# Own buffers for the first gate's second half of weights, and one ordering edge less, in a hybrid encoder block

## The chip, the cores and the metric

The kernel runs on one core of one Trainium2 chip. The metric is the time of one execution on the device in microseconds (us), taken over several runs; a separate profiled execution gives the trace. The engines are TensorE (PE; its weight loads are shown as PEld), VectorE (DVE), ScalarE (ACT), GpSimd (POOL) and SyncE (SP), which issues most of the DMA transfers.

## The reference, cut to what matters

A sequence of 1024 frames with 16 learned meta tokens ahead of it runs through one block: a token mixer with two groups of heads, then a gated MLP with a causal depthwise convolution, each added to the stream, and a last norm.

```python
h = concatenate([meta, x], axis=1)                     # (1, 1040, 1024)
h = h + token_mixer(rmsnorm(h, norm_mix_g), ...)
h = h + channel_mixer(rmsnorm(h, norm_ffn_g), ...)
return rmsnorm(h, norm_final_g)[:, 16:]

def channel_mixer(u, w_up, w_gate, ffn_conv_w, w_down):   # D_FF = 2816
    a = causal_dwconv(u @ w_up, ffn_conv_w)               # 3 taps
    return (silu(a) * (u @ w_gate)) @ w_down
```

The change lies at the start of channel_mixer: the norm of its input and the products with the first block of w_up and w_gate.

## The kernel before

Everything is held transposed: features on the 128 partitions, time along the free axis. The residual stream lies in eight blocks of 128 features (RES; tiles resid). Every float32 operand of a product is split into a high part that TensorE reads in one pass (fp32r, made by a cast on ACT) and the rest (lo, made by a subtraction on DVE), and each product is three matmuls: hi by hi, hi by lo, lo by hi (mm3s, lines 924 to 926). All weights go through wsplit: a cast on line 783, a subtraction on line 784.

The 22 blocks of 128 columns of D_FF are taken in eleven pairs. For pairs 1 to 10 the products follow Strassen's scheme with seven half-size products (seven; its products are named pup_x, pup_y, pup_z for w_up and pga_x, pga_y, pga_z for w_gate), which needs sums and differences of the input's quarters: the combinations. Pair 0 is done in the ordinary way (eight), before the combinations are there. A name such as pup_001 is the product of w_up for block 0 of pair 0, half 0 of the time, part 1; pga_11 that of w_gate for block 1, half 1.

The stretch around the change, in the order of the code:
- The last quarter of the token mixer's output product (pwy) is added to the stream in two pieces of 256 columns. The squares of each piece (sqb) are summed over the blocks (Rb, line 2060). The norm of a piece is a matmul that sums over the partitions (pcb, line 827), a square root and a reciprocal on two columns, a matmul that spreads the result over rows (prb, line 839) and a copy to Rb (line 843). Then scale_tasks multiplies the eight blocks by Rb (line 2070) and makes the split input: uh_g and x on ACT (line 1998), ul_g and x on DVE (line 1999). Half 1, the later half of the time, has had its norm before (tiles xh, xl).
- first_up and first_gate compute pair 0: half 1 first, then half 0 in two parts, 0 (columns up to 256) and 1 (the rest).
- xcomb(k, j0, j1) makes the combinations for one of four feature blocks k and one part of the columns; the first quarter's have j0 = 0. Each has an ACT scaling (line 2025), subtractions on DVE (lines 2026, 2029, 2031, 2034) and four splits (xput: lines 1995 to 1999) into uh_g, ul_g, xh and xl. Its temporaries are xu, xt, xv.
- Then come the pairs; conv takes the up-projection's blocks through three taps and Silu (lines 2238 to 2241, tiles cv), and gate multiplies by the gate's block (line 2283).

The order of instructions on each engine here is made by a scheduler in the framework, which runs the program against a model of its own and keeps to the dependencies. `after(a, b)` adds an edge for the order only. Buffers come from pools; a tile waits until the readers of the one that had its place are done. Three places matter:
- Split weights take turns in a ring of three pairs of tiles of 128x1024 (split_tiles: hi, lo). fstep(u, s) makes the s-th split of the u-th weight block; u = 0 is w_up and u = 1 w_gate of pair 0, and s is the block of 128 columns. hi_ga_1 and lo_ga_1 in the order below are the splits for (u, s) = (1, 1). The raw weights of w_gate are the tiles fraw_ga.
- ctile gives tiles of 128x512 from a ring of six with the tag "cv"; before the change only the convolutions use it. Its pool is opened where the pool with the tiles rr has just been closed, whose last readers are matmuls of pwy.
- xcomb orders the first subtraction of every combination except the very first behind the last scaling of the stream (last["scaled"], set on line 2071 by xsingle).

## Time and profile before

| | |
|---|---|
| median of 3 runs | 1526.14 us (1525.41 to 1527.58) |
| span of the profiled execution | 1523.9 us; the profile states no time for it beside the span |
| median less that span | 2.2 us |
| PE busy | 1487.8 us, 98% of the span |
| PEld, DVE, ACT, POOL busy | 1349.9, 1090.4, 756.4, 72.1 us |
| granted clock of TensorE over the span | 0.995 |
| transfers | 223.81 MB, mean 147 GB/s |
| chain that ended last | PE 89%, DVE 5%, ACT 2%, DMA 2%, issue 1% |

The span runs from the first to the last instruction; a run's time has what lies around it as well. A busy time is the union of an engine's instructions. In a row of the timeline stand the start, the time, the engine, the line, the operation with what it writes and reads, and in brackets the idle time of the engine before it and what ended that. The end of a matmul is modelled, so its length is more than its distance to the next one's start. In the list of waits stand the total, the number of times and the longest. The chain of waits is followed back from the end, each step with its start and length.

### The profile page before, as it was taken

The numbers are of one execution on the slowest core, as the hardware profiler recorded it, in microseconds if no ns is written. First come the engines' busy times: TensorE is split into PE (matmuls) and PEld (weight loads), VectorE is DVE, ScalarE is ACT, GpSimd is POOL, SyncE is SP. The second block draws the span as 40 slices with busy tenths as digits, with TensorE's granted clock in tenths as the row PEclk, the third lists the DMA queues.
The fourth block names the chain that finished last, engine by engine and source line by source line (L and its number), as shares of the span: only waits on it lengthen the run. The fifth ranks groups of instructions, "written<-read, shape, count | busy, mean of one in ns | idle before, by whom it ended". The sixth has DMA issues, their size and how long they took to land.

```text
span 1523.9 us, 25488 instructions
## 1 busy us (share of the span) xinstructions
PE 1487.8 (98%) x9929; PEld 1349.9 (89%) x9929; DVE 1090.4 (72%) x2087; ACT 756.4 (50%) x1455; POOL 72.1 (5%) x157
## 2 busy tenths in 40 slices
PE   7989999999999999999999999999999999999997
PEld 7988999998999999987888998999999999888887
DVE  6885868677777677756867787766666666778667
ACT  4465655554655455544454565444444444344443
POOL 1000000000000000000000001222220000000000
PEclk9999999999999999999999999999999999999999
DMA  6022245323632446697333247887772224933213
GB/s 232 2 93 56 90 155 192 111 84 111 200 106 98 131 161 199 194 401 258 108 115 125 77 136 222 209 211 201 177 186 77 83 82 157 369 106 108 97 42 111
DMA packets 104586, 223.81 MB, mean 147 GB/s; under 512 B 10520, under 2 KB 33760, under 8 KB 104288
## 3 DMA queue, kind: packets, MB, share of 16 engines
q1 hardware_dynamic: 89824, 191.68, 37.4%
q0 software_dynamic: 8448, 23.07, 7.6%
q10 hardware_dynamic: 6192, 7.41, 1.4%
q8 instruction: 78, 1.28, 0.3%
q14 instruction: 44, 0.36, 0.1%
HBM read 178.05 MB, written 67.15 MB: 161 GB/s over the span
## 4 chain that ended last, share of the span: by engine, by line
PE 89%; DVE 5%; ACT 2%; DMA 2%; issue 1%; SPq 0%; DVEq 0%; ACTq 0%
PE pdx L926 3%; PE pdx L925 3%; PE pdx L924 3%; PE pup_x L925 2%; PE pup_x L924 2%; PE pup_x L926 2%; PE pga_x L924 2%; PE pga_x L925 2%; PE pga_x L926 2%; PE pdy L926 2%; PE pdy L925 2%; PE pdy L924 2%; PE n L1621 2%; PE pwx L926 2%; PE u L1619 2%; PE pwx L924 2%
## 5 line engine op out<-in xcount | busy, mean ns | idle before, releaser
L783 ACT CAST hi_up<-raw_up 128x512 fp32r<-128x512 f32 (+1 forms) x52 | 36.4, 719 | 106.7 <-PE pga_z L925 60.2
L924 PE MATMUL pup_x<-uh_g,hi_up 128*128 128x256 f32 (+1 forms) x240 | 67.6, 284 | 1.2 <-ACT uh_g L1995 1.2
L784 DVE TENSOR_TENSOR lo_up<-raw_up,hi_up 128x512 fp32r<-128x512 f32 (+1 forms) x52 | 41.3, 809 | 38.3 <-ACT hi_up L783 37.5
L784 DVE TENSOR_TENSOR lo_ga<-fraw_ga,hi_ga 128x512 fp32r<-128x512 f32 (+1 forms) x52 | 41.9, 808 | 37.3 <-ACT hi_ga L783 37.1
L925 PE MATMUL pup_x<-ul_g,hi_up 128*128 128x256 f32 (+1 forms) x240 | 67.7, 284 | 0.1
L926 PE MATMUL pup_x<-uh_g,lo_up 128*128 128x256 f32 (+1 forms) x240 | 66.5, 283 | 0.0
L784 DVE TENSOR_TENSOR lo_d<-rd,hi_d 128x1024 fp32r<-128x1024 f32 (+1 forms) x34 | 37.7, 1113 | 32.8 <-ACT hi_d L783 32.7
L783 ACT CAST hi_ga<-fraw_ga 128x512 fp32r<-128x512 f32 (+1 forms) x52 | 36.4, 719 | 45.5 <-PE pup_z L925 24.1
L926 PE MATMUL pdx<-uh_d,lo_d 128*128 128x512 f32 (+1 forms) x156 | 57.9, 375 | 0.0
L925 PE MATMUL pdx<-ul_d,hi_d 128*128 128x512 f32 (+1 forms) x156 | 57.8, 374 | 0.0
L783 ACT CAST hi_d<-rd 128x1024 fp32r<-128x1024 f32 (+1 forms) x34 | 32.3, 959 | 49.3 <-PE pdy L925 32.5
L926 PE MATMUL pdy<-uh_d,lo_d 128*128 128x512 f32 x132 | 51.9, 393 | 0.0
L925 PE MATMUL pdy<-ul_d,hi_d 128*128 128x512 f32 x132 | 51.7, 392 | 0.0
L924 PE MATMUL pdx<-uh_d,hi_d 128*128 128x512 f32 (+1 forms) x156 | 48.5, 372 | 0.0
L924 PE MATMUL pdy<-uh_d,hi_d 128*128 128x512 f32 x132 | 47.9, 389 | 0.0
L924 PEld LDWEIGHTS pup_x<-uh_g,hi_up 128*128 128x128 f32 x240 | 45.7, 191 | 2.3 <-ACT uh_g L1995 1.4
L924 PE MATMUL pga_x<-uh_g,hi_ga 128*128 128x512 f32 x120 | 47.5, 396 | 0.0
L925 PE MATMUL pga_x<-ul_g,hi_ga 128*128 128x512 f32 x120 | 47.5, 396 | 0.0
L926 PE MATMUL pga_x<-uh_g,lo_ga 128*128 128x512 f32 x120 | 47.1, 393 | 0.0
L925 PEld LDWEIGHTS pup_x<-ul_g,hi_up 128*128 128x128 f32 x240 | 45.8, 191 | 1.0 <-DVE ul_g L1996 0.3
L926 PEld LDWEIGHTS pup_x<-uh_g,lo_up 128*128 128x128 f32 x240 | 45.0, 190 | 0.7
L1688 DVE SCALAR_TENSOR_TENSOR mx<-tr,vec,sig 128x386 f32<-128x386 f32 (+2 forms) x42 | 24.0, 571 | 21.1 <-PE tr L1680 16.0
(1687 smaller groups left out, 5732.4 us busy)
## 6 DMA issues: line engine op xcount, KB each, us to landing
raw_up<-w_up_d SPq DMA_DIRECT2D x22, 512.0 KB, 5.6
fraw_ga<-w_gate_d SPq DMA_DIRECT2D x22, 512.0 KB, 4.3
acts<-cv SPq DMA_DIRECT2D x44, 256.0 KB, 4.6
wsd<-w_down_d POOLq DMA_DIRECT2D x44, 256.0 KB, 6.7
rd<-wsd SPq DMA_DIRECT2D x22, 512.0 KB, 3.5
raw_w<-w_out_d SPq DMA_DIRECT2D x20, 512.0 KB, 7.3
wsw<-raw_w SPq DMA_DIRECT2D x32, 256.0 KB, 3.1
raw_m<-w_out_d SPq DMA_DIRECT2D x14, 512.0 KB, 4.0
```

Of the source, the lines that this page charges most:

```text
L783: AC.copy(hi[:, o:o + n], x)
L784: V.tensor_tensor(lo[:, o:o + n], x, hi[:, o:o + n].bitcast(F32), ALU.subtract)
L924: m.append(PE.matmul(pt, ah, xh_, start=first and k == 0, stop=False, skip_group_check=True))
L925: PE.matmul(pt, ah, xl_, start=False, stop=False, skip_group_check=True)
L926: m.append(PE.matmul(pt, al, xh_, start=False, stop=last and k == n - 1, skip_group_check=True))
L1619: PE.matmul(up[:, :nv], kw[:L], v, start=True, stop=True)
L1621: PE.matmul(pn[:L, :nv], pt[:L, :L], v, start=True, stop=c == 0)
L1688: return V.scalar_tensor_tensor(dst, tr[:, x0 - t0:x1 - t0], vec[:, g:g + 1], sig(b, p)[:, x0 - a0:x1 - a0], ALU.mult, ALU.mult)
```

## The change

The split for (u, s) = (1, 1), the second block of columns of pair 0's gate, no longer takes a place in the ring of weight tiles. It is made in two pieces of 512 columns, hi and lo each, in four tiles from the ring "cv" (higa_1_0, higa_1_1, loga_1_0, loga_1_1). Products of eight read the piece that holds their columns. And the edge in xcomb holds only for the second part of the columns (j0 > 0).

```diff
@@ fsplit, wsplit @@
+    def wsplit2(nm, x):
+        r = [[ctile(f"{p}{nm}_{i}", F32R) for i in range(2)] for p in ("hi", "lo")]
+        for i in range(2):
+            wsplit(r[0][i], r[1][i], [x[:, i * HB:(i + 1) * HB]])
+        return r
+
@@ fstep @@
+        if (u, s) == (1, 1):
+            return wsplit2(nm, r1)
         if u < 2:
             return fsplit(nm, [(r0, r1)[s]])
@@ xcomb @@
         x = V.scalar_tensor_tensor(t3, B1, g1, u4, ALU.mult, ALU.subtract)
-        if k or j0:
+        if j0:
             after(x, last["scaled"])
@@ eight @@
-            mm3s(pt, [tuple(y[:, kb * P:(kb + 1) * P] for y in (hi, lo)) for kb in range(KB)],
+            mm3s(pt, [tuple(y[kb // 4][:, kb % 4 * P:(kb % 4 + 1) * P] if type(y) is list else y[:, kb * P:(kb + 1) * P] for y in (hi, lo)) for kb in range(KB)],
                  [tuple(y[:, kb % 4, j0:j1] for y in xs[kb]) for kb in range(KB)], True, True)
```

The scheduler moves instructions by it on PE, DVE and ACT between the norm of the two last pieces and the products of pair 1; on SP one load moves; the rest of the program stands in the order of before. Lines from 788 on have numbers higher by 6 to 8 in the changed kernel.

On ACT, at the split of the first block of the gate's weights (hi_ga_0), before:

```order
L783 CAST hi_ga_0_9731<-fraw_ga_0_9422 128x1024
L2056 ACTIVATE sqb_3_9464<-resid_8123 128x256
L2056 ACTIVATE sqb_5_9504<-resid_8124 128x256
L2056 ACTIVATE sqb_6_9508<-resid_8125 128x256
L2056 ACTIVATE sqb_7_9512<-resid_8125 128x256
```

and in the changed kernel:

```order
L783 CAST hi_ga_0_9731<-fraw_ga_0_9422 128x1024
L783 CAST higa_1_0_9847<-fraw_ga_1_9424 128x512
L783 CAST higa_1_1_9848<-fraw_ga_1_9424 128x512
L2064 ACTIVATE sqb_3_9464<-resid_8123 128x256
L2064 ACTIVATE sqb_5_9504<-resid_8124 128x256
```

The casts of the second block stand ahead of the squares of the two last pieces; before, that cast (hi_ga_1) stood 31 rows further on, behind the scaling of both pieces. On DVE the two subtractions loga_1_0 and loga_1_1 likewise stand behind lo_ga_0 and ahead of the sums in Rb.

On PE, at the end of pga_01, the gate's product for block 0 and half 1, before:

```order
L926 MATMUL pga_01_9855<-xh_9052,lo_ga_0_9732 128x512
L924 MATMUL pup_000_9911<-uh_g,hi_up_0_9418 128x256
L924 MATMUL pup_100_9938<-uh_g,hi_up_1_9426 128x256
L925 MATMUL pup_000_9911<-ul_g,hi_up_0_9418 128x256
L926 MATMUL pup_000_9911<-uh_g,lo_up_0_9419 128x256
```

and in the changed kernel (pcb_9633 is the norm's sum for the last piece):

```order
L934 MATMUL pga_01_9859<-xh_9052,lo_ga_0_9732 128x512
L932 MATMUL pga_11_9887<-xh_9054,higa_1_0_9847 128x512
L933 MATMUL pga_11_9887<-xl_9055,higa_1_0_9847 128x512
L934 MATMUL pga_11_9887<-xh_9054,loga_1_0_9849 128x512
L835 MATMUL pcb_9633<-cs,Rb 128x1 x2
```

The 24 matmuls of pga_11 come directly behind pga_01. Before, they came behind pup_000, pup_100, pup_001 and pup_101, mixed with pga_00. Now the order behind them is pup_000 (with prb of the last piece after its first 12 matmuls), pup_100, pga_00, pga_10, pup_001, pup_101.

On DVE, at the last combinations of the second part (k = 3), around the product of the first convolution of pair 1 with its gate (cv_00<-s0ga,cv_00), before:

```order
L2283 TENSOR_TENSOR cv_00_10314<-s0ga_10339,cv_00_10314 128x512
L2026 SCALAR_TENSOR_TENSOR xt_256_10225<-resid_8123,vec,xv_256_10211 128x258
L2034 SCALAR_TENSOR_TENSOR xv_256_10211<-resid_8125,vec,xv_256_10211 128x258
L2029 SCALAR_TENSOR_TENSOR xt_256_10225<-resid_8123,vec,xt_256_10225 128x258
L2031 TENSOR_TENSOR xv_256_10211<-resid_8123 128x258
```

and in the changed kernel:

```order
L2034 SCALAR_TENSOR_TENSOR xt_256_10229<-resid_8123,vec,xv_256_10215 128x258
L2004 TENSOR_TENSOR ul_g<-xv_256_10215,uh_g 128x258
L2291 TENSOR_TENSOR cv_00_10318<-s0ga_10343,cv_00_10318 128x512
L2037 SCALAR_TENSOR_TENSOR xt_256_10229<-resid_8123,vec,xt_256_10229 128x258
L2039 TENSOR_TENSOR xv_256_10215<-resid_8123 128x258
L2042 SCALAR_TENSOR_TENSOR xv_256_10215<-resid_8125,vec,xv_256_10215 128x258
```

The first xt now stands ahead of that product, and one of the two xv has gone behind the second xt. On ACT, between the cast hi_up_3 of pair 1 and the load of the Silu table for that convolution stood one scaling, one cast and one copy (uh_g, uh_g, s2up); now one cast stands there (uh_g).

## The prediction

> **What bounds the kernel now.** I read the page first, then the list of PE's waits from 760 us on, then the busy times by stretches around the place that the change touches (columns after the stretch: PE, PE's weight loads, DVE, ACT, POOL, then the granted clock, the DMA share and GB/s).

> ```profile
> span 1523.9 us, 25488 instructions
> PE pup L925 <- DVE ul_g L1999: 1.7, 1, 1.7
> PE pup_x L924 <- ACT uh_g L1995: 1.2, 1, 1.2
> PE pga L924 <- ACT hi_ga L783: 0.8, 1, 0.8
> 870.00:875.00 5.00, 3.33 (x27) 3.00 (x25) 3.20 (x10) 3.11 (x8) 0.00 (x0) 1.00 0.00 0
> 880.00:885.00 5.00, 4.22 (x34) 3.93 (x33) 3.85 (x6) 2.00 (x2) 0.00 (x0) 1.00 0.22 57
> 915.00:920.00 5.00, 3.67 (x20) 3.09 (x19) 3.45 (x10) 2.43 (x7) 0.00 (x0) 0.83 0.90 301
> 920.00:925.00 5.00, 5.00 (x38) 5.00 (x37) 3.86 (x8) 2.30 (x5) 0.00 (x0) 0.83 0.55 211
> 930.00:1400.00 470.00, 470.00 (x2763) 415.68 (x2762) 324.78 (x497) 205.65 (x357) 52.37 (x74) 1.00 0.60 168
> ```

> TensorE is the bound: from 930 to 1400 us it is busy for all 470.00 us. So what the change can be worth is what PE loses between about 845 and 930 us, the start of the gated MLP. There it waits three times, and after the third wait the clock is 0.83 in two stretches of 5 us, which are 10 x 0.17 = 1.7 us lost. The column of idle time understates a stall, because the end of the matmul ahead of it is modelled. Start to start is the honest measure:

> ```profile
> 872.83 0.51 PE L924 MATMUL pup<-uh_g,hi_up 128*128 128x258 f32 x2
> 875.03 0.39 PE L925 MATMUL pup<-ul_g,hi_up 128*128 128x258 f32 x1 [1.69 <-DVE ul_g L1999]
> 875.25 0.28 PE L926 MATMUL pup<-uh_g,lo_up 128*128 128x258 f32 x1
> 875.37 0.29 PE L924 MATMUL pup<-uh_g,hi_up 128*128 128x258 f32 x1
> ...
> 880.52 0.28 PE L926 MATMUL pup<-x,lo_up 128*128 128x258 f32 x1
> 881.58 0.50 PE L924 MATMUL pga<-xh,hi_ga 128*128 128x512 f32 x1 [0.78 <-ACT hi_ga L783]
> 881.92 0.39 PE L925 MATMUL pga<-xl,hi_ga 128*128 128x512 f32 x1
> ...
> 914.90 0.28 PE L926 MATMUL pup_x<-uh_g,lo_up 128*128 128x258 f32 x1
> 916.37 0.39 PE L924 MATMUL pup_x<-uh_g,hi_up 128*128 128x258 f32 x1 [1.19 <-ACT uh_g L1995]
> 916.82 0.38 PE L924 MATMUL pup_z<-uh_g,hi_up 128*128 128x258 f32 x1
> 917.28 0.39 PE L925 MATMUL pup_x<-ul_g,hi_up 128*128 128x258 f32 x1
> 917.51 0.28 PE L926 MATMUL pup_x<-uh_g,lo_up 128*128 128x258 f32 x1
> ```

> An undisturbed matmul of 258 columns starts 0.12 us after the last (875.25 to 875.37), one of 512 columns 0.23 us. Stall 1: 872.83 to 875.25 is 2.42 us for three steps of 0.12, lost 2.06. Stall 2: 880.52 to 881.92 is 1.40 for one step of 0.12 and one of 0.23, lost 1.05. Stall 3: 914.90 to 917.51 is 2.61 for four steps, lost 2.13. Together 5.24 us, and 1.7 us of slow clock behind the third.

> **Edit one: the four buffers.** The split of the gate's second half (hi and lo of w_gate[0, 1]) took turns in the ring of weight tiles, and had to wait for the up-projection's last read. That is stall 2, with PE waiting for the cast. With own buffers the casts stand directly behind those of the first half, and PE's matmuls on them (24 of 512 columns, pga_11) stand directly behind pga_01 and not behind pup_001 and pup_101.

> ```profile
> 866.35 0.39 PE L926 MATMUL pga<-xh,lo_ga 128*128 128x512 f32 x1
> 866.58 0.40 PE L924 MATMUL pup<-uh_g,hi_up 128*128 128x256 f32 x2
> ...
> 870.91 0.46 PE prb L839 x4
> 871.39 0.38 ACT Rb L843
> 871.80 2.77 DVE resid L2070 x8
> 874.57 0.41 DVE ul_g L1999
> ```

> Stall 1 is the chain from the norm's rows (prb) over ACT's copy and eight scalings to the first low part: 870.91 to 875.03, 4.1 us. PE has too little other work for it: it starts pup_000 at 866.58 and is through by 872.83. Now 24 x 0.23 = 5.5 us of pga_11 come ahead, and pga_00 and pga_10 (48 matmuls of 254 columns, 5.7 us) move between prb and pup_001. By the new order the row matmul stands behind 12 matmuls of pup_000: 866.58 + 5.5 + 0.4 (the sum's matmul) + 12 x 0.12 = 874.0. Its low parts are then there at 874.0 + 4.1 = 878.1, or some 1.2 us later, since three combinations of about 0.4 us now stand among them on DVE. PE reaches pup_001 at 874.0 + 0.5 + 36 x 0.12 + 5.7 = 884.5. Margin 5 us: stall 1 goes wholly, 2.06 us.

> ```profile
> 844.30 0.81 SPq L772 DMA_DIRECT2D fraw_ga<-w_gate_d x2
> DMA to landing us min/median/max: 3.6/4.2/6.7
> 845.01 0.28 PE L926 MATMUL pwy<-rr,wl 128*128 128x256 f32 x1
> 848.08 1.05 ACT L783 CAST hi_ga<-fraw_ga 128x1024 fp32r<-128x1024 f32 x1 [1.46 <-DMA fraw_ga<-w_gate_d]
> 849.00:849.50 0.50, 0.50 (x6) 0.50 (x5) 0.50 (x3) 0.49 (x3) 0.00 (x0) 1.00 0.00 0
> 852.42 1.82 DVE L2060 TENSOR_TENSOR Rb<-Rb,sqb 128x256 f32<-128x256 f32 x4
> 855.72 0.50 PE L827 MATMUL pcb<-cs,Rb 128*128 128x1 f32 x4
> 880.48 1.04 ACT L783 CAST hi_ga<-fraw_ga 128x1024 fp32r<-128x1024 f32 x1 [0.92 <-PE pup L925]
> 913.99 0.69 DVE L2283 TENSOR_TENSOR cv<-s0ga,cv 128x512 f32<-128x512 f32 x1 [0.97 <-ACT cv L2241]
> ```

> The new casts wait for two things. One is the landing of the second half: issued at 844.7, and the DMA engines are idle from 849.0 on, while ACT is free at 848.08 + 1.05 = 849.1. The other is the memory of the tiles rr, which the new pool lies over; their last reader starts at 845.01. So the casts run at 849.1 instead of 880.48, and stall 2 goes: 1.05 us. The price is order, not work: two subtractions of 128x512 on DVE (0.69 us each, by the row of that size at 913.99) now precede the sums of squares. The last sum for the first quarter is done at 852.42 + 1.4 + 0.4 = 854.2; PE comes to its matmul (855.72 before, now 11 matmuls of 0.12 later) at 857.0. Hidden, by 2.8 us. If that cover went, PE would wait at pcb, with the rest of pup in order behind it. The split itself is the same work in two pieces. On SP one load (ga1's second half) is issued earlier, past one write of the stream; nothing waits for either then. The buffers come from the six of the convolutions' ring; they are free after pga_10, long before a third convolution asks.

> **Edit two: the combinations of the first quarter are not ordered behind the stream's scaling.** No work is added. Three more k of the combinations of columns 0 to 255 may run while PE does pga_11, and DVE and ACT (3.20 and 3.11 of 5 us busy in 870 to 875) have room. Everything behind is earlier, up to the combinations of the other half, whose last one is stall 3:

> ```profile
> 910.00 0.62 ACT L783 CAST hi_up<-raw_up 128x512 fp32r<-128x512 f32 x1 [1.27 <-PE pga_y L925]
> 912.04 1.28 ACT L2241 ACT_TABLE_LOAD   x1
> 914.60 0.48 DVE L2026 SCALAR_TENSOR_TENSOR xt<-resid,vec,xv 128x258 f32<-128x258 f32 x1
> 915.91 0.41 ACT L1995 CAST uh_g<-xt 128x258 fp32r<-128x258 f32 x1
> ```

> The cast that PE wants (915.91) hangs on xt, xt stands on DVE behind cv (913.99, above), and cv waits for ACT's load of the Silu table. That load begins 2.04 us after the cast at 910.00. In the new order one cast stands between them, 0.62 + 0.41 = 1.0 us, so it comes 1.0 earlier against PE. Behind cv stood three instructions up to the cast ((915.91 - 914.60) / 3 = 0.44 each); now it is one, the first xt having moved ahead of cv and xv behind: 0.87 earlier. The wait shrinks by 1.87 of 2.13 us and 0.26 is left, too little for the clock by what this trace shows: stall 1, 1.69 us in the idle column, left it at 1.00. The bounds of this term are 0 (the chain is as late as before) and 2.13.

> **The clock.** The profile shows one drop, 1.7 us, just after stall 3. Stall 1 was as long and brought none, so it seems to hang on where a stall falls. I take 1.2 us for the median run, between 0 (the runs that make the median had none) and 1.7, nearer to the one execution that is shown. [...]

> **Sum.** 2.06 + 1.05 + 1.87 = 4.98, and 1.2 of clock: 6.2 us. Against the profiled execution that is 1523.9 - 6.2 = 1517.7 of span. The median of the runs, 1526.14, is 2.2 above that span, launch and end around it; 1526.14 - 6.2 = 1519.9.

> **Rivals.** Bound of "no change" is 0.2%, 3.05 us, about what a measurement of this kernel can tell.
> (a) The stalls go, the median keeps or never had the slow clock: 1526.14 - 5.0 = 1521.1. For it: only one of two long stalls brought a drop. Against: the drop directly behind stall 3. [...]
> (b) Stall 3 stays whole, because table load and cast come as late against PE as before: 3.1 us gained, 1523.0. For it: that chain starts from PE's own progress (hi_up waits for pga_y). Against: the order, which takes instructions out of it.
> (c) The gain is given back later, or the casts stay late as the buffers are not free: about 1525.5. For it: the DMA share of 0.60 in 930 to 1400; weights asked for earlier may not land earlier. Against: PE waits for nothing in those 470 us.
> (d) Slower: the second half lands late and ACT, strictly in order, holds the squares behind the cast. With 2.8 us of slack it costs PE from a landing at about 852 on, each us later costing one; slower than before from 852 + 6.2 = 858, 13.5 us after its issue. The longest landing of these loads is 6.7 us. Price at 16 us: 1528.

> **How the numbers follow.** Forecast 0.56 (own range 1518.4 to 1521.8), (a) 0.20, (b) 0.12, (c) 0.08, (d) 0.04. Range 1518.4 to 1523.1: it reaches from a clock and a third stall won wholly, with another 0.8 for a second drop missed, up to (b); left out are (c), (d) and about 0.05 below. Faster takes the forecast, (a) and half of (b), which lies on the bound: 0.82. Same: half of (b) and (c), 0.14. Slower 0.04.

> **What would show it.** In the profile after: hi of ga's second half cast near 849 in two pieces; pga_11 behind pga_01; no wait of pup for ul_g, none of pga for hi_ga; the wait of pup_x for uh_g under 0.5 us; the clock 1.00 from 860 to 930; all that follows some 5 to 7 us earlier. Wrong if a new wait stands at pcb or prb, if pup_x still waits a microsecond, or if PE is no longer busy throughout after 930.

## The result, and the profile after

The changed kernel takes 1519.47 us (median of 5 runs, 1518.73 to 1521.55), the kernel before 1526.23 us beside it (median of 5 runs, 1525.41 to 1527.58). The ratio is 0.9957, 95% interval 0.9945 to 0.9968: 6.6 us less, 4.9 to 8.4. A second group of runs gave 1519.91 against 1525.86 us, ratio 0.9958 (0.9945 to 0.9970). Forecast were 1519.9 us and a profiled span of 1517.7; the span is 1517.0.

The head of the page and the stretches that were shown of before, from the profile of after (the columns as there). The list of TensorE's waits from 760 to 930 us, which had three rows before, is empty.

```profile
span 1517.0 us, 25491 instructions
PE 1484.8 (98%) x9929; PEld 1347.9 (89%) x9929; DVE 1089.9 (72%) x2088; ACT 755.9 (50%) x1456; POOL 72.2 (5%) x157
870.00:875.00 5.00, 5.00 (x37) 4.63 (x36) 4.26 (x12) 3.67 (x10) 0.00 (x0) 1.00 0.14 52
880.00:885.00 5.00, 5.00 (x44) 5.00 (x44) 4.96 (x15) 2.40 (x6) 0.00 (x0) 1.00 0.00 0
915.00:920.00 5.00, 5.00 (x44) 5.00 (x43) 4.80 (x9) 1.81 (x5) 0.00 (x0) 1.00 0.66 234
920.00:925.00 5.00, 5.00 (x28) 4.28 (x27) 4.26 (x8) 4.97 (x11) 1.87 (x4) 1.00 0.61 174
930.00:1400.00 470.00, 470.00 (x2762) 415.70 (x2762) 325.78 (x498) 205.46 (x356) 50.67 (x72) 1.00 0.59 165
```

PE is busy for all 5.00 us where it had 3.33, 4.22 and 3.67, and the granted clock is 1.00 where it was 0.83. Behind 930 us nothing has changed: still 470.00 of 470.00 us.

To weigh the change apart from the rest of the program I take two matmuls that every kernel here has: the first of the norm's column sums (pcb) and the first of pga_z. From the timeline of PE, of before (first two rows) and of after:

```profile
831.55 0.39 PE L827 MATMUL pcb<-cs,Rb 128*128 128x1 f32 x3
930.77 0.40 PE L924 MATMUL pga_z<-uh_g,hi_ga 128*128 128x512 f32 x1
```

```profile
831.10 0.95 PE L835 MATMUL pcb<-cs,Rb 128*128 128x1 f32 x8
923.87 0.40 PE L932 MATMUL pga_z<-uh_g,hi_ga 128*128 128x512 f32 x1
```

The stage between them went from 99.22 to 92.77 us. What lies ahead of it (the front) is 0.45 us shorter by chance, what lies behind it (the tail) is 593.1 us in both. In the table below, "stage" is that distance of starts in each kernel's trace; front and tail are the rest of its span.

| kernel | front | stage | tail | time, median | ratio to before, 95% interval |
|---|---|---|---|---|---|
| before | 831.6 | 99.2 | 593.1 | 1526.23 | |
| after | 831.1 | 92.8 | 593.1 | 1519.47 | 0.9957 (0.9945 to 0.9968) |
| after, second group | 831.5 | 92.8 | 593.1 | 1519.91 | 0.9958 (0.9945 to 0.9970) |
| buffers alone | 833.3 | 97.4 | 593.1 | 1525.99 | 0.9996 (0.9987 to 1.0005) |
| edge alone | 833.7 | 99.2 | 593.1 | 1527.27 | 1.0001 (0.9992 to 1.0009) |
| before, early Silu table | 834.1 | 96.6 | 593.1 | 1525.45 | 0.9986 (0.9977 to 0.9995) |
| after, early Silu table | 835.9 | 92.5 | 593.6 | 1523.44 | 0.9967 (0.9956 to 0.9978) |
| the same, second group | 832.4 | 92.5 | 593.4 | 1520.06 | 0.9959 (0.9945 to 0.9972) |
| buffers, early Silu table | 831.5 | 96.7 | 593.1 | 1523.60 | 0.9982 (0.9974 to 0.9991) |
| after, casts six times | 833.6 | 92.5 | 593.1 | 1519.35 | 0.9958 (0.9945 to 0.9970) |
| after, load three times | 833.7 | 92.9 | 593.0 | 1520.64 | 0.9954 (0.9939 to 0.9968) |
| after, load five times | 833.6 | 92.4 | 593.8 | 1520.42 | 0.9952 (0.9935 to 0.9969) |

The kernel before, beside these, took 1526.98 us (rows four to seven), 1525.86 (second groups, casts, buffers with early table) and 1528.36 (the two last). The front moves by up to 4.8 us with no relation to the edits; the stage is the same within 0.05 us when a kernel is traced twice. So the stage tells kernels apart that the times hardly do. (A ratio here is not the quotient of the two medians in the table; the two differ by up to 0.001.)

### The profile page after: what moved, and what is told of

The parts are those of the page before. It is cut to its first block, busy times and chain, and to the rows that moved or that the text cites. A ratio compares the mean times of both kernels' runs of the same rounds, so it can differ in the third digit from the quotient of the medians.

```text
span 1517.0 us, 25491 instructions
## 1 busy us (share of the span) xinstructions
PE 1484.8 (98%) x9929; PEld 1347.9 (89%) x9929; DVE 1089.9 (72%) x2088; ACT 755.9 (50%) x1456; POOL 72.2 (5%) x157
## 3 DMA queue, kind: packets, MB, share of 16 engines
q8 instruction: 78, 1.28, 0.4%
## 4 chain that ended last, share of the span: by engine, by line
PE 90%; DVE 5%; ACT 2%; DMA 1%; issue 1%; SPq 0%; DVEq 0%; ACTq 0%
PE pdx L934 3%; PE pdx L933 3%; PE pdx L932 3%; PE pup_x L933 3%; PE pup_x L932 3%; PE pup_x L934 3%; PE pga_x L932 2%; PE pga_x L933 2%; PE pga_x L934 2%; PE pdy L934 2%; PE pdy L933 2%; PE pdy L932 2%; PE n L1629 2%; PE pwx L934 2%; PE u L1627 2%; PE pwx L932 2%
## 5 line engine op out<-in xcount | busy, mean ns | idle before, releaser
L783 ACT CAST hi_up<-raw_up 128x512 fp32r<-128x512 f32 (+1 forms) x52 | 36.4, 719 | 108.2 <-PE pga_z L933 61.1
L783 ACT CAST hi_ga<-fraw_ga 128x512 fp32r<-128x512 f32 (+1 forms) x51 | 35.4, 713 | 44.6 <-PE pup_z L933 23.9
L783 ACT CAST hi_d<-rd 128x1024 fp32r<-128x1024 f32 (+1 forms) x34 | 32.3, 959 | 49.3 <-PE pdy L933 32.5
```

The source lines that it names most:

```text
L783: AC.copy(hi[:, o:o + n], x)
```

## The experiments

### Each edit alone

The first edit without the second: the edge of before is put back into the changed kernel.

```diff
-        if j0:
+        if k or j0:
             after(x, last["scaled"])
```

> The first edit alone: four buffers for the first gate's second half, the edge behind the stream's scaling kept for every k and j0. The prediction's attribution: stalls 1 and 2 go (3.1 us of the span), stall 3 and the clock drop behind it stay, since the combinations still wait for the scaling: 1526.2 - 3.1 = 1523.1 us, range 1522.5 to 1523.8. A second theory: with stalls 1 and 2 gone TensorE comes earlier to the combinations while ScalarE's chain in front of them (copies, table load, casts) has not moved, so part of what was saved is waited out there: stall 3 grows from 2.1 to about 3.4 us and only 1.7 us are kept, about 1524.5 us. Rival: the buffers alone carry the whole gain, 1519.5 us, with no wait at the combinations and no clock drop.

Measured: 1525.99 us, ratio 0.9996 (0.9987 to 1.0005); stage 97.4, so 1.9 us of the 6.4. PE's waits from 760 to 935 us in this kernel, and the rows of PE at stall 3 (rows between left out):

```profile
PE pup_x L932 <- ACT uh_g L2003: 1.1, 1, 1.1
PE pup_z L932 <- ACT uh_g L2006: 0.7, 1, 0.7
```

```profile
912.86 0.28 PE L934 MATMUL pup_x<-uh_g,lo_up 128*128 128x256 f32 x1
913.80 0.38 PE L932 MATMUL pup_z<-uh_g,hi_up 128*128 128x258 f32 x1 [0.66 <-ACT uh_g L2006]
...
916.52 0.39 PE L932 MATMUL pup_x<-uh_g,hi_up 128*128 128x258 f32 x1 [1.13 <-ACT uh_g L2003]
...
917.81 0.42 PE L934 MATMUL pup_x<-uh_g,lo_up 128*128 128x258 f32 x1
```

Stalls 1 and 2 are gone. But PE now waits at the combinations twice: 912.86 to 917.81 is 4.95 us for ten steps of 0.12, so 3.75 lost, about 0.2 of it because the clock fell before the last two. Stall 3 was 2.13 and is some 3.5. The second theory holds: 3.1 us saved, 1.4 waited out later; 1.7 kept, where the stage shows 1.9. The times alone do not show this gain: their interval reaches from 2.0 us less to 0.8 us more. The clock dropped to 0.50 behind it (916.94 to 920.36 us), as in before (918.28 to 921.69). What held the combinations is seen on DVE, in the timeline at the scaling of the last piece, first with the buffers alone, then in the changed kernel:

```profile
876.47 2.78 DVE L2078 TENSOR_TENSOR resid<-resid,Rb 128x256 f32<-128x256 f32 x8 [3.38 <-ACT Rb L851]
```

```profile
874.24 2.77 DVE L2078 TENSOR_TENSOR resid<-resid,Rb 128x256 f32<-128x256 f32 x8 [0.37 <-ACT Rb L851]
```

With the edge DVE stands idle for 3.38 us before the scaling, because the combinations are ordered behind it; without the edge it does one more k in that time (idle 0.37). Counted on ACT, the writes of uh_g in 35 us from the same point of the program (each stretch begins 18.4 to 18.5 us behind the first pcb), in before, in after and with the buffers alone (busy time of these writes, in brackets their number, then clock, DMA share and GB/s):

```profile
850.00:885.00 35.00, 5.89 (x14) 1.00 0.18 57
```

```profile
849.50:884.50 35.00, 8.34 (x20) 1.00 0.21 72
```

```profile
851.80:886.80 35.00, 6.71 (x16) 1.00 0.23 71
```

The second edit without the first, made in the kernel before:

```diff
-        if k or j0:
+        if j0:
             after(x, last["scaled"])
```

> The second edit alone: the edge is only set for j0 > 0, the first gate's second half keeps the shared buffers. TensorE's order is then that of before; a group of combinations moves ahead of four scalings on VectorE and ScalarE. Theory: all three stalls stay (1.7, 1.2 and 0.8 us of waits in the trace of before), 1526.2 us within 1 us, since without the buffers TensorE has nothing to run in front of the combinations. Rival: the edge alone lets the combinations of the first quarter be ready earlier and stall 3 shrinks by 1.9 us as in the changed kernel, with the clock drop gone too: 1522.7 to 1524.3 us.

Measured: 1527.27 us, ratio 1.0001 (0.9992 to 1.0009), stage 99.2, and PE's three waits to the tenth:

```profile
PE pup L925 <- DVE ul_g L1999: 1.7, 1, 1.7
PE pup_x L924 <- ACT uh_g L1995: 1.2, 1, 1.2
PE pga L924 <- ACT hi_ga L783: 0.8, 1, 0.8
```

The edge alone is worth nothing, though one k does run ahead of the scaling with it: DVE's idle time there, 3.59 us in before, is 0.88 (first row below). What stops the rest is xh. The last split of every combination overwrites the block of xh that pga_11, the gate's product for block 1 and half 1, reads. Without buffers of its own pga_11 stands behind stall 2, so ACT's cast into xh waits 3.17 us for a matmul of pga, until 887.84 us (second row); it does so in before too, for the same 3.17 us, until 885.65. The scalings for the next k stand behind this cast on ACT; in before the first of them starts at 886.65.

```profile
873.99 2.77 DVE L2070 TENSOR_TENSOR resid<-resid,Rb 128x256 f32<-128x256 f32 x8 [0.88 <-ACT Rb L843]
887.84 0.41 ACT L1995 CAST xh<-xv 128x256 fp32r<-128x256 f32 x1 [3.17 <-PE pga L926]
```

In the changed kernel pga_11 comes directly behind pga_01, and the same cast waits for its own operand alone:

```profile
870.00 0.41 ACT L2003 CAST xh<-xv 128x256 fp32r<-128x256 f32 x1 [2.80 <-DVE xv L2042]
```

So two things hold the combinations, the edge and xh, and each edit frees one of them. The third k of the first quarter starts on DVE 55.6 us behind the first pcb in before and with the edge alone, 52.0 with the buffers alone and 45.8 with both. That is why the two edits don't add: 0 and 1.9 us alone, 6.4 together.

### The link of stall 3, and the clock

The kernel before with the Silu table loaded early, by a tiny Silu behind the last square root. The order on PE, DVE, POOL and SP stays as it was; on ACT the table load goes from in front of the first convolution's Silu to about 868 us.

```diff
+    early = tmp.tile([P, 5], F32, tag="rcol", name="early")
+    after(AC.activation(early[:, 0:1], epsc, AF.Silu), last["sqrt"])
```

> The kernel before, with one tiny Silu (128x1) on ScalarE right behind the last Sqrt, so that the table load of 1.28 us stands at about 867 us and no longer between ScalarE's copy and the casts that the combinations wait for in stall 3. Theory (the table load is the link of stall 3, and the stall sets off the clock drop): stalls 1 and 2 stay, stall 3 shrinks by 1.1 to 1.28 us to about 0.9, and with so short a stall the granted clock does not fall: 1.1 + 1.7 less, 1523.4 us; if the clock falls all the same, 1525.1 us. Rival: another link (the copy, the last matmul of a gate) ends last, and the table load is only beside it: no change, 1526.2 us.

Measured: 1525.45 us, ratio 0.9986 (0.9977 to 0.9995), stage 96.6. The row of the load, which began at 912.04 us in before, and PE's rows at stall 3, from the timeline of this kernel; then the stretch in which before had a clock of 0.83:

```profile
867.87 1.28 ACT L2180 ACT_TABLE_LOAD   x1
...
917.44 0.28 PE L926 MATMUL pup_x<-uh_g,lo_up 128*128 128x258 f32 x1
917.85 0.39 PE L924 MATMUL pup_x<-uh_g,hi_up 128*128 128x258 f32 x1
918.28 0.38 PE L924 MATMUL pup_z<-uh_g,hi_up 128*128 128x258 f32 x1
918.76 0.39 PE L925 MATMUL pup_x<-ul_g,hi_up 128*128 128x258 f32 x1
918.98 0.28 PE L926 MATMUL pup_x<-uh_g,lo_up 128*128 128x258 f32 x1
```

```profile
915.00:920.00 5.00, 4.74 (x35) 4.13 (x35) 4.50 (x12) 2.42 (x7) 0.00 (x0) 1.00 0.84 249
```

The same five matmuls took 2.61 us from first to last start in before and take 1.54 here: stall 3 is 1.07 us shorter, and 1.06 us of it is left. The granted clock stayed at 1.00 from 880 to 930 us. Stalls 1 and 2 are as in before. The stage is 2.6 us shorter, so the clock was worth 2.6 - 1.07 = 1.5 us. That agrees with what a half-clock stretch costs by its matmuls, here with the buffers alone (a stretch of the windows with PE's busy time first, PEld, DVE, ACT and POOL behind it, and then the clock; and two rows of the timeline, nine steps of one shape apart):

```profile
913.53:916.94 3.41, 1.90 (x7) 1.15 (x7) 3.41 (x10) 2.27 (x6) 0.00 (x0) 1.00 0.79 246
916.94:920.36 3.42, 3.40 (x14) 3.22 (x15) 1.66 (x5) 0.68 (x2) 0.00 (x0) 0.50 0.84 265
920.36:923.77 3.41, 3.41 (x31) 3.41 (x30) 2.54 (x5) 1.69 (x4) 0.00 (x0) 1.00 0.90 326
```

```profile
918.02 0.42 PE L932 MATMUL pup_z<-uh_g,hi_up 128*128 128x256 f32 x1
...
919.95 0.41 PE L932 MATMUL pup_z<-uh_g,hi_up 128*128 128x256 f32 x1
```

Nine steps in 1.93 us are 0.214 us each against 0.12: in 3.41 us that loses 3.41 x (1 - 0.12 / 0.214) = 1.5 us. The time of this run is a weak witness (the interval holds 0.8 to 3.5 us); the trace is the evidence.

The buffers alone with the early table (both edits of code as shown above):

> The first edit alone (buffers, edge kept) with the Silu table loaded early. In the trace with the buffers alone TensorE still waits 0.7 and 1.1 us at the combinations and the stage is 97.36. Theory one (the edge): the combinations stand behind the stream's scaling on VectorE, the table load is only beside it; the stage shrinks by 0.8 us at most, to 96.5, with the clock still at half for 3.4 us. Theory two (the table load): with the load out of the way the waits go and the stage comes to 93 to 94 us, the edge being worth little.

Measured: 1523.60 us, ratio 0.9982 (0.9974 to 0.9991); stage 96.7, as theory one said (96.5). PE still waits, by its list of waits, and the clock falls, by a stretch of the windows:

```profile
PE pup_x L932 <- ACT uh_g L2003: 1.3, 2, 1.1
914.50:917.91 3.41, 3.40 (x15) 3.13 (x16) 1.46 (x4) 0.68 (x2) 0.00 (x0) 0.50 0.94 290
```

So the table load is a link of stall 3 worth 0.7 to 1.1 us in kernels that have the edge. What takes the stall away in the changed kernel is mainly that the combinations are early.

### The changed kernel with the early table

> The changed kernel with the same early Silu. The residue of stall 3 (0.29 us in the trace of after) is all that the table load can still cost: 1519.5 - 0.3 = 1519.2 us, range 1518.7 to 1519.7. Rival: a Silu table loaded early makes a later table load necessary or delays the sums of squares that TensorE waits for at the norm: 1 us or more slower.

Measured: 1523.44 us, ratio 0.9967 (0.9956 to 0.9978), where 1519.2 was expected: read by the time alone, the rival. The stage says otherwise: 92.5, 0.3 us less than the changed kernel, as expected. In the traced run, which took 1523.74 us, the loss is in the front, 835.9 us, ahead of anything that the edits touch. It was run once more beside the changed kernel, on another chip.

> The changed kernel with the Silu table loaded early, beside the changed kernel itself. Its stage was 92.49 us against 92.78, so 0.3 us less than the changed kernel is expected on the same chip; rival: the 1523.44 us of its first group (1518.78 to 1524.04) come from the early load, and it is 2 to 4 us slower than the changed kernel here too.

> The changed kernel once more, beside the kernels of this group on one chip. The stage from the first matmul of the norm's column sums (pcb, near 831 us) to the first matmul of pga_z (near 924 us) took 99.22 us in the trace of before and 92.78 in that of after; the part behind it 593.1 in both. Theory: the change acts in this stage alone, and what lies ahead of it differs from run to run whatever the kernel: stage 92.8 again, 6.4 us below the kernel before within the spread of 1 to 2 us. Rival: part of the 6.76 us measured was luck of the stretch ahead of 831 us or the stage depends on the run: stage between 93.5 and 97.

Measured: 1520.06 us for the early table and 1519.91 for the changed kernel; stages 92.5 and 92.8. The first group's loss is so put down to the front, which one trace of that group shows. The 0.3 us in the stage do not show in the time, so this is no better version that could be told apart. The changed kernel's stage is the same to 0.05 us in the second trace: its gain is not luck of one trace.

### The price of the new casts, and a late landing

Each new cast done six times over:

```diff
         for i in range(2):
+            for _ in range(5):
+                AC.copy(r[0][i], x[:, i * HB:(i + 1) * HB])
             wsplit(r[0][i], r[1][i], [x[:, i * HB:(i + 1) * HB]])
```

> The changed kernel with each of the two new casts of the second half done six times over (the same values again; ten casts of about 0.53 us more on ScalarE, 5.3 us in all) ahead of the norm's sums of squares. The prediction's slack was 2.8 us: where the squares are held up by the whole 5.3 us, TensorE waits 2.5 us at the column sums and the stage grows from 92.8 to 95.3 us. Rival: the order of ScalarE's and VectorE's work gives way (squares and scalings go in between the casts), and nothing is lost: 92.5 to 92.9 us.

Measured: 1519.35 us, ratio 0.9958 (0.9945 to 0.9970), stage 92.5, no wait of PE. The casts went in between the squares and the copies; the last of them, in ACT's timeline:

```profile
861.51 0.62 ACT L783 CAST higa<-fraw_ga 128x512 fp32r<-128x512 f32 x1
```

The rival holds: the order gives way. Twelve casts in place of two cost nothing.

The load of the second half issued three times and five times in a row, each waiting for the last:

```diff
-            nc.sync.dma_start(t[:, :2 * HB], fsrc[kind][i, j])
+            for _ in range(1 + n * ((u, j) == (1, 1))):     # n = 2 and 4
+                nc.sync.dma_start(t[:, :2 * HB], fsrc[kind][i, j])
```

> The changed kernel with the load of the first gate's second half issued three times in a row (each waits for the last), so that the half lands later; it landed at about 849 us in the trace of after, and should land near 857 here. The prediction's fourth rival put the slack at a landing of 852 us and a loss from 858 us on, because ScalarE's casts would hold the squares. Theory: the casts come behind the squares, and TensorE reads the half only at 865.7 us, so nothing is lost: stage 92.5 to 92.9 us. Rival: the squares or the matmuls of pga_11 wait: stage 93.5 to 96 us.

> The same with the load issued five times, landing near 865 us, where TensorE begins to read the half at 865.7 us in the trace of after. The casts and subtractions are 1.1 + 0.7 us behind the landing, so TensorE comes to pga_11 some 1 to 2 us too early unless other matmuls go first. Theory: this is past the slack, stage 93.5 to 95 us with a wait of TensorE for higa or loga. Rival: other matmuls take its place and nothing is lost, 92.5 to 92.9 us; or the loads behind it on SP's queue come late too and the stalls of the kernel before return, 96 to 99 us.

Measured: 1520.64 and 1520.42 us, ratios 0.9954 (0.9939 to 0.9968) and 0.9952 (0.9935 to 0.9969); stages 92.9 and 92.4. With three loads PE waits once, 0.2 us at prb for the norm's reciprocal. With five loads ACT's first cast and PE's first matmul on it are:

```profile
867.12 0.62 ACT L784 CAST higa<-fraw_ga 128x512 fp32r<-128x512 f32 x1 [4.82 <-DMA fraw_ga<-w_gate_d]
868.57 0.40 PE L933 MATMUL pga<-xh,higa 128*128 128x512 f32 x1
```

The front of this trace is 2.45 us longer than that of after, so the landing at 867.1 is 864.7 there, 15.7 us later than the 848.9 of after, and costs nothing. For five loads the rival with other matmuls in front was right and my theory, a stage of 93.5 to 95, wrong. Both times the program was ordered with the late landing in view; a landing that is late by surprise, with the order of the changed kernel kept, was not tried.

## Why the prediction was right, point by point

**Stall 1 (2.06 us, goes wholly).** Right. PE comes to pup_001 at 883.59 us (forecast 884.5), and the low parts are made from 877.33 on (forecast 878.1):

```profile
877.33 1.67 DVE L2007 SCALAR_TENSOR_TENSOR ul_g<-resid,vec,uh_g 128x258 fp32r<-128x258 f32 x4
883.59 0.29 PE L932 MATMUL pup<-uh_g,hi_up 128*128 128x258 f32 x1
```

**Stall 2 (1.05 us, goes).** Right. The casts run at 848.93, forecast 849.1, though they waited 0.25 us for the landing, which the forecast had put as done:

```profile
847.63 1.05 ACT L783 CAST hi_ga<-fraw_ga 128x1024 fp32r<-128x1024 f32 x1 [1.46 <-DMA fraw_ga<-w_gate_d]
848.93 1.14 ACT L783 CAST higa<-fraw_ga 128x512 fp32r<-128x512 f32 x2 [0.25 <-DMA fraw_ga<-w_gate_d]
```

**The price hidden, slack 2.8 us at pcb.** Right: the first row of sums below ends the norm's sum for that piece with its first instruction, at 853.16 + 0.42 = 853.6, and PE comes at 856.60, 3.0 us later. How far the slack reaches was underrated, since I held the order fixed.

```profile
853.16 0.76 DVE L2068 TENSOR_TENSOR Rb<-Rb,sqb 128x256 f32<-128x256 f32 x2
856.60 0.50 PE L835 MATMUL pcb<-cs,Rb 128*128 128x1 f32 x4
```

**Stall 3 (2.13 us, shrinks by 1.87, 0.26 left).** Right in size: 0.31 and 0.22 us in place of two steps of 0.12 leave 0.29. The chain is the one named: from the cast of hi_up to the table load 0.95 us (906.44 to 907.39), forecast 1.0, where it was 2.04.

```profile
906.44 0.62 ACT L783 CAST hi_up<-raw_up 128x512 fp32r<-128x512 f32 x1 [1.18 <-PE pga_y L933]
907.39 1.28 ACT L2249 ACT_TABLE_LOAD   x1
...
911.59 0.28 PE L932 MATMUL pup_z<-uh_g,hi_up 128*128 128x258 f32 x1
911.90 0.39 PE L933 MATMUL pup_x<-ul_g,hi_up 128*128 128x258 f32 x1
912.12 0.28 PE L934 MATMUL pup_x<-uh_g,lo_up 128*128 128x258 f32 x1
```

**The clock (1.2 us).** The term that was mis-sized, by little: 1.5. Stalls of 5.24 - 0.29 = 4.95 and 1.5 of clock are 6.45; the stage shows 6.45. The 1.7 read from two stretches of 0.83 took half the clock for half the work. Rival (a), a median without the drop, finds no support: the drop stands behind stall 3 in every trace that has a stall of 2 us or more there (0.50 for 3.41 us in before and with the buffers without and with the early table; 0.66 over 920 to 925 us with the edge alone), and in none of the others (1.00 from 910 to 930 us in after, and with the early table in before and in after; the stages of the rest, 92.4 to 92.9 us, leave no room for 1.5 us). So 2.1 us of stall there were enough, and the 1.06 us left in before with the early table were not. But stall 1, 2.06 us long, brought no drop in any of the three traces that have it (in before the clock is 1.00 from 870 to 915 us). What fits all of these is how much was lost within one window of 3.413 us of the grid in the last section, if that grid runs on between the drops, counted by the starts as above: 2.12 to 2.57 us in the windows ahead of the four drops (914.87 to 918.28 in before), but 1.2 us in each of the two windows that stall 1 lies over in before (870.49 to 877.32), 1.3 and 1.1 with the edge alone, and 1.7 in the fuller of them in before with the early table. Ahead of this stage a wait of 2.4 us near 122 us kept the clock in one trace and lost it in another (last section), so no exact limit follows.

**Which edit does what.** This step failed: edit one was credited with stalls 1 and 2 (3.1 us) and edit two with stall 3. The runs gave 1.9 and 0 alone. Stall 1's and 2's time comes back at stall 3 unless the combinations come forward too, and for that both edits are needed: one lets them stand in front of the scaling, the other frees xh for them early. Of the three more k that the prediction saw beside pga_11, one ran in front of the scaling. The sum was right because the order of the changed kernel, with both edits in it, was what it was read from. That the median came within 0.5 us of the forecast is in part luck: the interval of the gain is 3.5 us wide.

**Rivals (b), (c) and (d).** No gain was given back after 930 us; stall 3 did not stay. The point set for (d), a loss from a landing at 858 us, was too early by at least 6.7 us wherever the order knows of it.

## What to carry to other kernels

Two waits on one engine that stand in a row are not two gains: taking the first away only brings the engine earlier to the second, unless the producers of the second are set free as well (here 1.4 of 3.1 us were waited out again). Where two things hold such a producer, freeing one can show nothing, and then two edits that are worth 1.9 and 0 us alone can be worth 6.4 together. Measure a stage between two instructions that all versions share; it held to 0.05 us where times of whole runs moved by 2 to 5. Removing a short stall can bring more than its own length where the clock falls behind it: here 1.5 us of clock stood behind stall 3's 2.13 us.

## What the runs showed of the hardware that was not expected

```profile
PE s L1574 <- DVE pt L1598: 2.4, 1, 2.4
110.00:130.00 20.00, 17.59 (x124) 1.00 0.47 106
```

```profile
PE s L1582 <- DVE pt L1606: 2.4, 1, 2.4
110.00:130.00 20.00, 17.61 (x115) 0.91 0.45 105
```

The number of such stretches ahead of 831 us (two in after, four in the early table's first group, at 1.5 us each), with some waits whose length differs between runs (1.6 to 3.1 us for the one near 122 us), accounts for most of what moved the front; by a rough sum of these two, up to 1.6 us is left over. At a granted clock of 0.50 matmuls of 256 columns start 0.214 us apart (buffers alone, 918.02 to 919.95 us) and not 0.24, 1.8 times as far as at full clock: half the clock did not cost half the work here.
